# Ten gate units of a decoder layer take a fourth pair by seven products, and 15 of their weight sums are formed in the mixer

## The chip, the cores and the metric

One core of a Trainium2 chip runs one whole decoder layer. The metric is the device time of one execution in microseconds (us). TensorE (PE in the profile) multiplies, VectorE (DVE) and ScalarE (ACT) convert and combine, GpSimd (POOL) and SyncE (SP) issue most of the transfers (DMA).

## What is computed

The layer has 256 tokens of 2048 features, in float32:

```python
h = rms_norm(x, ln_mix_pre);  q, k, v (two groups of 8 heads) = split(h @ w_in)      # w_in 2048 x 6144
o = rms_norm_per_head(concat(stick_breaking(q, k, v), dilated_mixture(q, k, v, bias)))
x = x + rms_norm(o @ w_out, ln_mix_post)                                             # 2048 x 2048
g, u = split(rms_norm(x, ln_ffn_pre) @ w_gate_up)                                    # 2048 x 11264
x = x + rms_norm((silu(g) * u) @ w_down, ln_ffn_post)                                # 5632 x 2048
x = x + sigmoid(rms_norm(x, ln_pli) @ w_pli_gate) * (p @ w_pli_proj)
```

## The kernel before

**Products.** Every float32 operand of a matmul is split into a high part (`hi`, cast to fp32r by ScalarE, L107) and a low part (`lo`, what is left, subtracted by VectorE, L108). A product is then three matmuls: hi by hi, hi by lo, lo by hi. A matmul takes a stationary tile of 128 x 128 (activations) and a moving one of 128 x 512 (weights) and adds into one of eight PSUM banks.

**Weights** come by SyncE's queue into `wraw`, are cast into `whi` and subtracted into `wlo`. Each of the three names is a ring of three buffers (`wp`, L80), so a tile is written when the users of the third one before it on its ring are done.

**Stages.** The mixer projects q, k and v chunk by chunk (`Chunk`, L131; `gemm`, L177; a group of four 128-row chunks of 512 columns is 24 matmuls, L157), with the work of the heads put between by a queue of small steps: `tick` (L117), called after each two chunks, runs the next step of `pending`. Then come w_out, the FFN in three parts (units 0 to 3, 4 to 7 and 8 to 10 of the gate, each part followed by two units of w_down), and the gate of the layer embedding.

**Pairs.** From w_out on, a unit computes two halves of 512 columns for both token tiles, and goes through the rows in pairs of chunks (`Pair`, L272). A plain pair is a 2 x 2 by 2 x 2 block product in eight products, 24 matmuls. A *seven* does it in seven products of sums and differences (after Strassen and Winograd), 21 matmuls. For that the activations' differences are made once (`sT`, by `differences`, L828), and for each pair four sums of its four weight blocks (`wsum`, one buffer, L288): one add of 1024 columns (L289) and two of 512 (L291, L292) on VectorE. Three products use the weights themselves, so three of the four blocks of `wraw` are split as they are (1536 columns, a `whi` and a `wlo`); four products use the sums, which are cast in two halves (L295, L296) and subtracted (L297) into another `whi` and another `wlo`. A seven so takes two buffers of each ring. Of a unit's eight pairs, 1, 3 and 5 are sevens (`SEVENS`, L30). Pairs 6 and 7 are always plain: after pair 5 the unit's product banks are combined (a copy by ScalarE, L409, and four adds by VectorE, L410 to L413) while the last two pairs go bank by bank, each bank ending with an add (L428), then silu (L360) or the product with it (L363).

**The order of the work** on each engine is fixed when the kernel is built: a list scheduler puts the emitted instructions in order, by priorities (weights stand 200 ahead, the chain that closes a unit 1000 ahead) and its own estimate of when operands are there. The same list decides on TensorE whether, for a tile that it expects late, all hi by hi products stand ahead of the first product that needs `wlo`. On the chip each engine keeps this order and waits for semaphores.

**p**, the layer embedding, is loaded once (L721) in the mixer by SyncE, split, and kept to the end of the kernel.

Of the kernel before, what the change touches and what calls it, by code (L numbers as in the profile page):

```python
# [34 lines left out]
def kernel(
# [234 lines left out]
    sums_pool = []  # L270

    class Pair:  # L272


        def __init__(self, src, na, nb, i, seven=False, row0=0, pieces=1):
            self.i, self.seven = i, seven
            with tc.high_priority(offset=WEIGHT_AHEAD):
# [11 lines left out]
                nc.vector.tensor_tensor(  # L289
                    s[:, 0:2], raw[:, 0:1].to_broadcast([P, 2, NB]), raw[:, 1:4:2], ALU.add)  # L290
                nc.vector.tensor_tensor(s[:, 2], s[:, 0], raw[:, 3], ALU.add)  # L291
                nc.vector.tensor_tensor(s[:, 3], s[:, 2], raw[:, 2], ALU.add)  # L292
# [716 lines left out]
```

## Time and profile before

| | |
|---|---|
| median of 3 runs | 1239.58 us (1239.23 to 1240.94) |
| profiled execution: time, span | 1239.78 us, 1238.1 us |
| granted TensorE clock | 0.999 |
| DMA, mean over the span | 198 GB/s |

The profile's page comes from one execution. The busy time of an engine is given with its share of the span; a group of instructions has its line, engine, operation and tiles (out<-in), count, busy time, mean ns of one, and what ended the idle time before it; a row of the timeline has the start in us from the span's start, the duration, and in brackets the idle time before and who ended it. Rows of windows have, after start:end and the length, the busy time and count of PE, PEld (weight loads), DVE, ACT, POOL, then the granted clock, the DMA share and GB/s. Rows of waits have the total, the count and the longest. Rows of DMA issues have count, size of one and the median time from issue to landing.

### The profile page before, as it was taken

The numbers are of one execution on the slowest core, as the hardware profiler recorded it, in microseconds if no ns is written. First come the engines' busy times: TensorE is split into PE (matmuls) and PEld (weight loads), VectorE is DVE, ScalarE is ACT, GpSimd is POOL, SyncE is SP. The second block draws the span as 40 slices with busy tenths as digits, with TensorE's granted clock in tenths as the row PEclk, the third lists the DMA queues.
The fourth block names the chain that finished last, engine by engine and source line by source line (L and its number), as shares of the span: only waits on it lengthen the run. The fifth ranks groups of instructions, "written<-read, shape, count | busy, mean of one in ns | idle before, by whom it ended". The sixth has DMA issues, their size and how long they took to land.

```text
span 1238.1 us, 14380 instructions
## 1 busy us (share of the span) xinstructions
PE 1227.1 (99%) x5496; PEld 990.4 (80%) x5496; DVE 965.4 (78%) x1007; ACT 659.7 (53%) x749; POOL 32.3 (3%) x57
## 2 busy tenths in 40 slices
PE   9999999999999999999999999999999999999997
PEld 6888888888888888888788788888888888887886
DVE  6575564545668968988888798899888988888886
ACT  6654554445444756555544555555464555655553
POOL 0001000000100200000000000000000000001000
PEclk9999999999999999999999999999999999999999
DMA  9845745555557845556455555655555665657661
GB/s 339 276 147 168 255 146 162 168 170 170 191 167 251 297 152 191 182 202 227 155 193 207 181 193 204 217 170 190 205 176 198 204 222 169 245 173 241 241 202 70
DMA packets 123301, 245.11 MB, mean 198 GB/s; under 512 B 7088, under 2 KB 7392, under 8 KB 122848
## 3 DMA queue, kind: packets, MB, share of 16 engines
q1 hardware_dynamic: 120448, 232.84, 55.6%
q0 software_dynamic: 2528, 11.02, 2.4%
q8 instruction: 43, 0.70, 0.2%
q10 hardware_dynamic: 256, 0.32, 0.1%
q14 instruction: 26, 0.21, 0.0%
HBM read 238.91 MB, written 6.83 MB: 198 GB/s over the span
## 4 chain that ended last, share of the span: by engine, by line
PE 93%; DVE 3%; DMA 1%; issue 1%; ACT 1%; POOL 0%; DVEq 0%; SPq 0%; ACTq 0%; POOLq 0%
PE bank L323 65%; PE bank L157 23%; DVE wlo L108 1%; PE bank L334 1%; PE bank L575 1%; DMA wraw<-in_w_down_dram 1%; PE bank L235 1%; PE bank L545 1%; DMA wraw<-in_w_in_dram 1%; ACT whi L107 1%; DMA y_sb<-in_xT_dram 0%; PE bank L588 0%; PE bank L587 0%; PE bank L586 0%; DVE temp L428 0%
## 5 line engine op out<-in xcount | busy, mean ns | idle before, releaser
L108 DVE TENSOR_TENSOR wlo<-wraw,whi 128x2048 fp32r<-128x2048 f32 (+3 forms) x229 | 463.6, 2033 | 162.5 <-ACT whi L107 161.6
L107 ACT CAST whi<-wraw 128x2048 fp32r<-128x2048 f32 (+3 forms) x229 | 389.7, 1704 | 330.9 <-PE bank L323 213.5
L323 PE MATMUL bank<-whi,hT_hi 128*128 128x512 f32 x667 | 262.5, 397 | 0.0
L323 PE MATMUL bank<-wlo,hT_hi 128*128 128x512 f32 x667 | 261.9, 395 | 0.0
L323 PE MATMUL bank<-whi,hT_lo 128*128 128x512 f32 x667 | 261.7, 395 | 0.0
L157 PE MATMUL bank<-whi,hT_hi 128*128 128x512 f32 x384 | 156.6, 409 | 1.2 <-ACT whi L107 1.2
L157 PE MATMUL bank<-wlo,hT_hi 128*128 128x512 f32 x384 | 152.0, 396 | 0.3 <-DVE wlo L108 0.3
L157 PE MATMUL bank<-whi,hT_lo 128*128 128x512 f32 x384 | 152.0, 396 | 0.0
L323 PEld LDWEIGHTS bank<-wlo,hT_hi 128*128 128x128 f32 x667 | 125.2, 188 | 30.8 <-DVE wlo L108 0.4
L323 PEld LDWEIGHTS bank<-whi,hT_lo 128*128 128x128 f32 x667 | 125.2, 188 | 29.9
L323 PEld LDWEIGHTS bank<-whi,hT_hi 128*128 128x128 f32 x667 | 125.2, 188 | 29.8
L297 DVE TENSOR_TENSOR wlo<-wsum,whi 128x2048 fp32r<-128x2048 f32 x50 | 114.5, 2290 | 23.8 <-ACT whi L296 23.8
L323 PE MATMUL bank<-wlo,fT_hi 128*128 128x512 f32 x282 | 111.0, 396 | 1.0 <-DVE wlo L108 1.0
L323 PE MATMUL bank<-whi,fT_hi 128*128 128x512 f32 x282 | 111.0, 396 | 0.0
L323 PE MATMUL bank<-whi,fT_lo 128*128 128x512 f32 x282 | 110.8, 396 | 0.0
L157 PEld LDWEIGHTS bank<-whi,hT_lo 128*128 128x128 f32 x384 | 72.3, 188 | 17.7 <-DVE hT_lo L493 0.2
L157 PEld LDWEIGHTS bank<-whi,hT_hi 128*128 128x128 f32 x384 | 72.3, 188 | 16.8 <-ACT whi L107 1.7
L157 PEld LDWEIGHTS bank<-wlo,hT_hi 128*128 128x128 f32 x384 | 72.4, 189 | 15.1 <-DVE wlo L108 1.1
L295 ACT CAST whi<-wsum 128x1024 fp32r<-128x1024 f32 x50 | 52.6, 1052 | 41.6 <-PE bank L323 28.4
L289 DVE TENSOR_TENSOR wsum<-wraw 128x1024 f32<-128x1024 f32 x50 | 61.0, 1221 | 6.7 <-DMA wraw<-in_w_down_dram 3.1
L323 PEld LDWEIGHTS bank<-wlo,fT_hi 128*128 128x128 f32 x282 | 53.0, 188 | 14.1 <-DVE wlo L108 1.5
L323 PEld LDWEIGHTS bank<-whi,fT_hi 128*128 128x128 f32 x282 | 53.0, 188 | 12.7
(193 smaller groups left out, 1437.4 us busy)
## 6 DMA issues: line engine op xcount, KB each, us to landing
wraw<-in_w_gate_up_dram SPq DMA_DIRECT2D x176, 512.0 KB, 4.8
wraw<-in_w_down_dram SPq DMA_DIRECT2D x88, 512.0 KB, 5.2
wraw<-in_w_in_dram SPq DMA_DIRECT2D x40, 1024.0 KB, 5.2
wraw<-in_w_pli_gate_dram SPq DMA_DIRECT2D x32, 512.0 KB, 5.1
wraw<-in_w_out_dram SPq DMA_DIRECT2D x8, 1024.0 KB, 5.0
wraw<-in_w_out_dram SPq DMA_DIRECT2D x16, 512.0 KB, 4.9
wraw<-in_w_in_dram SPq DMA_DIRECT2D x14, 512.0 KB, 8.5
y_sb<-in_x_dram SPq DMA_DIRECT2D x4, 512.0 KB, 10.2
```

Of the source, the lines that this page charges most:

```text
L107: nc.scalar.copy(hi, raw)
L108: nc.vector.tensor_tensor(lo, raw, hi.bitcast(F32), ALU.subtract)
L157: nc.tensor.matmul(self.pm[t], lhsT=a[:, c, t, :], rhs=b[:, c % KG, :], start=c == 0 and a is a_hi and b is hi, stop=c == self.nk - 1 and ...
L235: nc.tensor.transpose(out=pt[:, k * P:(k + 1) * P], in_=x_sb[c][:, t, k * P:(k + 1) * P], identity=ident)
L289: nc.vector.tensor_tensor(s[:, 0:2], raw[:, 0:1].to_broadcast([P, 2, NB]), raw[:, 1:4:2], ALU.add)
L295: nc.scalar.copy(shi[:, 0:2], s[:, 0:2])
L297: nc.vector.tensor_tensor(slo, s, shi.bitcast(F32), ALU.subtract)
L323: nc.tensor.matmul(pm, lhsT=a[u], rhs=w[v], start=first and x == 0 and y == 0, stop=last and x == len(terms) - 1 and y == 2)
L334: nc.tensor.transpose(out=pt[:, c * P:(c + 1) * P], in_=f[:, c * P:(c + 1) * P], identity=ident)
L545: nc.tensor.transpose(out=pt[:, h * P:(h + 1) * P], in_=nat[:, h * P:(h + 1) * P], identity=ident)
L575: nc.tensor.matmul(out, lhsT=a[u], rhs=b[w], start=i == 0, stop=i == 2)
```

## The change

1. **A fourth seven.** The gate units 1 to 10 take pairs 1, 2, 4 and 5 as sevens, not 1, 3 and 5. `sT` has room for four. Unit 0, w_out, w_down and the last gate stay as they are.
2. **Sums formed early.** For pair 1 of units 1 to 10 and pair 4 of the even ones, 15 sets in all, the sums are formed in the mixer. `first_sums` puts six steps for each set on a second queue (`aside`), of which `tick` runs one a call: load the four blocks by two transfers on POOL's queue into half of `y_sb`; nothing; four adds of 128x512 on VectorE; a store of 1 MB on POOL's queue into memory; nothing, twice. All sets use the one buffer. In the gate units such a pair loads its sums (1 MB, SyncE) and only three blocks of its weights (0.75 MB), and has no adds; its sums lie in another order (`swap`).
3. **p is loaded twice,** by POOL's queue: in w_out for its first use and in the third part of the FFN for its second; it isn't kept between.

The diff's core (line numbers shift: L295, L296, L297 become L337, L338, L339; L289 is L331 for the units' own sums; L409 is L452; L323 is L366; L107 and L108 stay; the early adds are L289, their loads L284, their stores L303):

```diff
+GATE_SEVENS = (1, 2, 4, 5)
+FIRST_SUMS = [(j, 1) for j in range(1, DFF // NB)] + [(j, 4) for j in range(2, DFF // NB, 2)]
...
-    pT_hi = const.tile([P, 2, T, P], F32R, name="pT_hi")
-    pT_lo = const.tile([P, 2, T, P], F32R, name="pT_lo")
...
+    def load_p(pool, raw):
+
+        nc.gpsimd.dma_start(out=raw.rearrange("q (k m) -> q k m", k=2), in_=pT)
+        p_split[:] = [pool.tile([P, 2, T, P], F32R, name=f"pT_{n}") for n in ("hi", "lo")]
+        split(*(a.rearrange("q k t m -> q (k t m)") for a in p_split), raw)
...
-    pending = deque()
+    pending, aside = deque(), deque()
...
             clock[0] += 1
+            if aside:
+                aside.popleft()()
...
+    def load_pair(queue, raw, src, rows, na, nb):
+        for n0, sl in ((nb, slice(0, 4, 3)), (na, slice(1, 3))):
+            queue.dma_start(out=raw[:, sl], in_=src[rows, n0:n0 + NB].rearrange("(c q) n -> q c n", q=P))
+
+    def first_sums(buf):
+
+        def add(o, u, v):
+            nc.vector.tensor_tensor(buf[:, o], buf[:, u], buf[:, v], ALU.add)
+
+        for j, i in FIRST_SUMS:
+            def load(j=j, i=i):
+                load_pair(nc.gpsimd, buf, w_gate_up, slice(i * 2 * P, (i + 1) * 2 * P), j * NB, DFF + j * NB)
+
+            def form():
+                add(1, 0, 1)
+                add(0, 0, 3)
+                add(3, 1, 3)
+                add(2, 3, 2)
+
+            def store(j=j, i=i):
+                sums_d[j, i] = dram.tile([P, 4, NB], F32, name=f"sums{j}_{i}")
+                nc.gpsimd.dma_start(out=sums_d[j, i], in_=buf)
+
+            idle = lambda: None
+            aside.extend((load, idle, form, store, idle, idle))
...
-            self.i, self.seven = i, seven
+            self.i, self.seven, self.swap = i, seven, 1 if sums is not None else 0
...
+                if sums is not None:
+                    nc.sync.dma_start(out=raw[:, 1:3], in_=src[rows, na:na + NB].rearrange("(c q) n -> q c n", q=P))
+                    nc.sync.dma_start(out=raw[:, 3], in_=src[rows.start + P:rows.stop, nb:nb + NB])
+                else:
+                    load_pair(nc.sync, raw, src, rows, na, nb)
...
+                if sums is not None:
+                    nc.sync.dma_start(out=s, in_=sums)
+                else:
+                    nc.vector.tensor_tensor(
+                        s[:, 0:2], raw[:, 0:1].to_broadcast([P, 2, NB]), raw[:, 1:4:2], ALU.add)
+                    nc.vector.tensor_tensor(s[:, 2], s[:, 0], raw[:, 3], ALU.add)
+                    nc.vector.tensor_tensor(s[:, 3], s[:, 2], raw[:, 2], ALU.add)
...
+            wi = wi if m < 4 else wi ^ self.swap
...
-        sevens = SEVENS[np]
+        sevens = sevens or SEVENS[np]
...
-            w = Pair(src, na, nb, i, seven, row0)
+            w = Pair(src, na, nb, i, seven, row0, sums=sums.get(i))
...
-            differences(sT)
+            differences(sT, GATE_SEVENS)
...
-        def load_late():
-
-            pT_sb = y_sb[:, 0, 0:NB]
-            with tc.high_priority(offset=WEIGHT_AHEAD):
-                nc.sync.dma_start(out=pT_sb.rearrange("q (k m) -> q k m", k=2), in_=pT)
-
-            later(lambda: split(*(a.rearrange("q k t m -> q (k t m)") for a in (pT_hi, pT_lo)), pT_sb))
...
-                if grp and base:
-                    load_late()
                 q = project_T(n0, rsq, "qT", before=load_norm if first else None)
+                if first:
+                    first_sums(y_sb[:, 0].rearrange("q (s n) -> q s n", n=NB))
...
-        sT = tuple(hxp.tile([P, 4, NS, P], F32R, name=f"sT_{n}") for n in ("hi", "lo"))
+        sT = tuple(hxp.tile([P, 4, len(GATE_SEVENS), P], F32R, name=f"sT_{n}") for n in ("hi", "lo"))
...
         load_x1(xsp, 0)
+        load_p(xsp, xsp.tile([P, NB], F32, name="p_raw"))
...
-                unit_seven(hT, sT, w_gate_up, j * NB, DFF + j * NB, KC // 2, out)
+                unit_seven(hT, sT, w_gate_up, j * NB, DFF + j * NB, KC // 2, out, sevens=GATE_SEVENS,
+                           sums={i: d for (jj, i), d in sums_d.items() if jj == j})
...
             load_x2(xs2, 0)
+            load_p(xs2, temp())
```

Three places show what moves. On ScalarE, the casts at the end of gate unit 2, before (whi_3961 and whi_3992 are pairs 4 and 5, whi_4002 the sums of pair 5, whi_4038 and whi_4045 pairs 6 and 7):

```order
L107 CAST whi_3961<-wraw_3960 128x2048
L107 CAST whi_3992<-wraw_3991 128x1536
L295 CAST whi_4002<-wsum_3996 128x1024
L296 CAST whi_4002<-wsum_3996 128x1024
L107 CAST fS_hi_3314<-temp_3848 128x4x128
L107 CAST whi_4038<-wraw_4037 128x2048
L409 COPY temp_4028<-bank4_73 128x512
L107 CAST whi_4045<-wraw_4044 128x2048
```

and after (whi_4092 are the sums of pair 4, whi_4119 pair 5, whi_4129 its sums, whi_4165 and whi_4172 pairs 6 and 7):

```order
L337 CAST whi_4092<-wsum_4088 128x1024
L338 CAST whi_4092<-wsum_4088 128x1024
L107 CAST whi_4119<-wraw_4118 128x1536
L337 CAST whi_4129<-wsum_4123 128x1024
L107 CAST whi_4165<-wraw_4164 128x2048
L452 COPY temp_4155<-bank4_73 128x512
L338 CAST whi_4129<-wsum_4123 128x1024
L107 CAST whi_4172<-wraw_4171 128x2048
L107 CAST whi_4237<-wraw_4236 128x2048
```

The cast of pair 6 and the copy now stand between the two halves of pair 5's sums. In the odd units from 3 on the copy stands ahead of the cast of pair 6, and in unit 1 that cast comes behind both halves.

On TensorE, the products of pair 5 in the same unit, before (hi by hi, lo, hi by lo in turn):

```order
L323 MATMUL bank3_72<-whi_3992,sT_hi_2731 128x512
L323 MATMUL bank3_72<-wlo_3993,sT_hi_2731 128x512
L323 MATMUL bank3_72<-whi_3992,sT_lo_2732 128x512
L323 MATMUL bank2_71<-whi_4002,sT_hi_2731 128x512
L323 MATMUL bank2_71<-wlo_4003,sT_hi_2731 128x512
L323 MATMUL bank2_71<-whi_4002,sT_lo_2732 128x512
L323 MATMUL bank1_70<-whi_4002,hT_hi_2726 128x512
L323 MATMUL bank1_70<-wlo_4003,hT_hi_2726 128x512
L323 MATMUL bank1_70<-whi_4002,hT_lo_2727 128x512
L323 MATMUL bank6_75<-whi_4002,sT_hi_2731 128x512
L323 MATMUL bank6_75<-wlo_4003,sT_hi_2731 128x512
L323 MATMUL bank6_75<-whi_4002,sT_lo_2732 128x512
```

and after:

```order
L366 MATMUL bank3_72<-whi_4119,sT_hi_2846 128x512
L366 MATMUL bank3_72<-wlo_4120,sT_hi_2846 128x512
L366 MATMUL bank3_72<-whi_4119,sT_lo_2847 128x512
L366 MATMUL bank2_71<-whi_4129,sT_hi_2846 128x512
L366 MATMUL bank6_75<-whi_4129,sT_hi_2846 128x512
L366 MATMUL bank0_69<-whi_4165,hT_hi_2841 128x512
L366 MATMUL bank7_76<-whi_4165,hT_hi_2841 128x512
L366 MATMUL bank3_72<-whi_4165,hT_hi_2841 128x512
L366 MATMUL bank1_70<-whi_4129,hT_hi_2841 128x512
L366 MATMUL bank5_74<-whi_4129,sT_hi_2846 128x512
L366 MATMUL bank2_71<-wlo_4130,sT_hi_2846 128x512
L366 MATMUL bank2_71<-whi_4129,sT_lo_2847 128x512
```

Seven hi by hi products, four with pair 5's sums and three with pair 6, stand ahead of the first one that needs wlo_4130, the low half of pair 5's sums; it is so in all ten units.

On VectorE, weight splits of the mixer between the heads' normalizations and the k projection of the next group, before:

```order
L108 TENSOR_TENSOR wlo<-wraw,whi 128x2048
L600 TENSOR_SCALAR d_1471<-ssh 128x2
L608 TENSOR_SCALAR tmp<-bank_75,rs_1473 128x128 x2
L108 TENSOR_TENSOR wlo<-wraw,whi 128x2048
L552 TENSOR_TENSOR kT<-bank_73,kT 128x4x128
L552 TENSOR_TENSOR kT<-bank_74,kT 128x4x128
L108 TENSOR_TENSOR wlo<-wraw,whi 128x2048
```

and after (the adds L289 are those of the sets 10 and 11):

```order
L289 TENSOR_TENSOR y_sb<-y_sb 128x512 x4
L108 TENSOR_TENSOR wlo<-wraw,whi 128x2048
L643 TENSOR_SCALAR d_1525<-ssh 128x2
L651 TENSOR_SCALAR tmp<-bank_75,rs_1527 128x128 x2
L108 TENSOR_TENSOR wlo<-wraw,whi 128x2048
L595 TENSOR_TENSOR kT<-bank_73,kT 128x4x128
L595 TENSOR_TENSOR kT<-bank_74,kT 128x4x128
L289 TENSOR_TENSOR y_sb<-y_sb 128x512 x4
L108 TENSOR_TENSOR wlo<-wraw,whi 128x2048
```

Each set's four adds stand between splits of weights, and VectorE reaches the splits behind them only when they are done.

More of the change, by code (lines that the diff above doesn't have):

```diff
@@ L268, with __init__ @@
     pp_d = dram.tile([P, T * D // 2], F32, name="pp_d")
-    sums_pool = []
+    sums_pool, sums_d = [], {}
+    def load_pair(queue, raw, src, rows, na, nb):
[17 more added lines that the diff above has]
+            aside.extend((load, idle, form, store, idle, idle))
     class Pair:
-        def __init__(self, src, na, nb, i, seven=False, row0=0, pieces=1):
-            self.i, self.seven = i, seven
+        def __init__(self, src, na, nb, i, seven=False, row0=0, pieces=1, sums=None):
+            self.i, self.seven, self.swap = i, seven, 1 if sums is not None else 0
             with tc.high_priority(offset=WEIGHT_AHEAD):
@@ L279, in __init__ @@
                 rows = slice(row0 + i * 2 * P, row0 + (i + 1) * 2 * P)
-                for n0, sl in ((nb, slice(0, 4, 3)), (na, slice(1, 3))):
-                    nc.sync.dma_start(
-                        out=raw[:, sl], in_=src[rows, n0:n0 + NB].rearrange("(c q) n -> q c n", q=P))
+                if sums is not None:
[3 more added lines that the diff above has]
+                    load_pair(nc.sync, raw, src, rows, na, nb)
                 self.w = (hi, lo)
@@ L288, in __init__ @@
                 s = sums_pool[-1].tile([P, 4, NB], F32, name="wsum")
[L289 to L292, printed above, removed]
+                if sums is not None:
[5 more added lines that the diff above has]
+                    nc.vector.tensor_tensor(s[:, 3], s[:, 2], raw[:, 2], ALU.add)
                 split(hi[:, 1:4], lo[:, 1:4], raw[:, 1:4])
@@ L392, in unit_seven @@
     def unit_seven(aT, sT, src, na, nb, np, out, row0=0, order=(2, 4, 8, 3), base=None, dest=None, ahead=None,
-                   M=BANKS, hold=None, between=None):
-        sevens = SEVENS[np]
+                   M=BANKS, hold=None, between=None, sevens=None, sums={}):
+        sevens = sevens or SEVENS[np]
         for i in range(np - 2):
             seven = i in sevens
-            w = Pair(src, na, nb, i, seven, row0)
+            w = Pair(src, na, nb, i, seven, row0, sums=sums.get(i))
             for m in (1, 2, 3, 5, 4, 7, 6) if seven else order:
@@ L803 @@
             nc.vector.tensor_tensor(o, u, v, op)
-            split(sT[0][:, i], sT[1][:, i], o)
+            split(sT[0][:, i, 0:NS], sT[1][:, i, 0:NS], o)
         for n in range(2):
@@ L826, in temp, with differences, laid @@
         return ffn2.tile([P, NB], F32, name="temp")
-    def differences(sT):
-        yv = y_sb.rearrange("q t (i f) -> q t i f", f=NB)
-        a1, a2, a3, a4 = (yv[:, t, 0:NS, (2 + c) * P:(3 + c) * P] for t in range(T) for c in range(2))
+    def differences(sT, sevens):
+        n = len(sevens)
+        if n == 4:
+            step = sevens[2] - sevens[0]
+            yv = y_sb[:, :, sevens[0] * 2 * P:(sevens[0] + 2 * step) * 2 * P].rearrange(
+                "q t (a b c m) -> q t a b c m", a=2, b=step, m=P)[:, :, :, 0:2]
+            a1, a2, a3, a4 = (yv[:, t, :, :, c] for t in range(T) for c in range(2))
+        else:
+            yv = y_sb.rearrange("q t (i f) -> q t i f", f=NB)
+            a1, a2, a3, a4 = (yv[:, t, 0:n, (2 + c) * P:(3 + c) * P] for t in range(T) for c in range(2))
+        def laid(x):
+            return x.rearrange("q (a b) m -> q a b m", a=2) if n == 4 else x
         box = {}
@@ L836, in run @@
                 u1, v1 = box.get(u, None) if isinstance(u, int) else u, v
-                box[i] = temp()[:, 0:NS * P].rearrange("q (i m) -> q i m", m=P)
+                box[i] = laid(temp()[:, 0:n * P].rearrange("q (i m) -> q i m", m=P))
                 nc.vector.tensor_tensor(box[i], u1, v1, op)
-                split(sT[0][:, i], sT[1][:, i], box[i])
+                split(laid(sT[0][:, i]), laid(sT[1][:, i]), box[i])
             return run
@@ L847, in embed @@
     def embed(na, banks, out, loaded=None):
-        unit_plain((pT_hi, pT_lo), w_pli_proj, na, na + NB, 1, banks, out, loaded=loaded)
+        unit_plain(p_split, w_pli_proj, na, na + NB, 1, banks, out, loaded=loaded)
     proj = []
@@ L942, in normed @@
         rs.extend(token_rs(lambda t, c: x_sb[c][:, t], t) for t in range(T))
-        differences(sP)
+        differences(sP, SEVENS[8])
     unit_plain(hT, w_pli_gate, 0, NB, KC // 2, {(0, 0): 1, (0, 1): 7, (1, 0): 2, (1, 1): 6}, evac_gate(0), front=2,
```

1 line of the change is left out of this document (added).

## Prediction

> **What bounds the kernel now.** I read the busy table of the page first, then what TensorE waited for, then one stage in a window.
>
> ```profile
> span 1238.1 us, 14380 instructions
> PE 1227.1 (99%) x5496; PEld 990.4 (80%) x5496; DVE 965.4 (78%) x1007; ACT 659.7 (53%) x749; POOL 32.3 (3%) x57
> ...
> PE bank L204 <- DVE junk L201: 1.3, 1, 1.3
> PE bank L157 <- ACT whi L107: 1.2, 1, 1.2
> PE bank L323 <- DVE wlo L108: 1.0, 1, 1.0
> ...
> 200.00:300.00 100.00, 100.00 (x484) 82.02 (x483) 52.84 (x72) 47.59 (x71) 2.76 (x4) 1.00 0.51 165
> 700.00:800.00 100.00, 100.00 (x439) 80.78 (x438) 87.10 (x80) 55.90 (x50) 0.00 (x0) 1.00 0.58 196
> ```
>
> TensorE is busy all the time, at granted clock 1.00 (the column after POOL's), and its longest wait is 1.3 us. So a matmul less is time less, and a wait that is new is time more: nothing else has to give way. VectorE (DVE) is 52.84% busy in a mixer window and 87.10% in a gate window; ScalarE (ACT) about half. The profiled execution took 1239.8 us, 0.2 above the median of the runs; I sum against 1239.8. About 0.2% (2.5 us) is what a measurement can tell from no change.
>
> **Fewer matmuls.** The pitch of matmuls is read from two rows of TensorE's timeline, 48 matmuls with nothing between:
>
> ```profile
> 614.29 0.39 PE L323 MATMUL bank<-whi,fT_hi 128*128 128x512 f32 x1
> ...
> 625.25 0.40 PE L323 MATMUL bank<-whi,fT_lo 128*128 128x512 f32 x1
> ```
>
> They start 47 pitches and 10.96 us apart: 0.2333 us each. Ten pairs go from 24 matmuls to 21, 30 x 0.2333 = **-7.0 us**, all on the path. A plain pair is 5.6 us of TensorE; a seven's own weights (h) are 9 matmuls, 2.1 us, and its sums (s) 12 matmuls, 2.8 us.
>
> **The end of a gate unit.** A whi tile has three buffers, and a seven takes two of them (h and s). In a gate unit after the change the tiles follow each other as p0, h1, s1, h2, s2, p3, h4, s4, h5, s5, p6, p7, and a tile can be written when TensorE is done with the third before it. p6 so waits for s4. Before, the last seven was followed by two plain pairs as well, but what stood ahead of its h was a plain pair of 5.6 us; now it is another seven. What each step takes:
>
> ```profile
> L108 DVE TENSOR_TENSOR wlo<-wraw,whi 128x2048 fp32r<-128x2048 f32 x151 | 345.8, 2290 | 150.3 <-ACT whi L107 149.7
> L107 ACT CAST whi<-wraw 128x2048 fp32r<-128x2048 f32 x151 | 288.4, 1910 | 280.9 <-PE bank L323 168.5 <-PE bank L157 67.5 <-issue 42.4
> L297 DVE TENSOR_TENSOR wlo<-wsum,whi 128x2048 fp32r<-128x2048 f32 x50 | 114.5, 2290 | 23.8 <-ACT whi L296 23.8
> L289 DVE TENSOR_TENSOR wsum<-wraw 128x1024 f32<-128x1024 f32 x50 | 61.0, 1221 | 6.7 <-DMA wraw<-in_w_down_dram 3.1 <-DMA wraw<-in_w_gate_up_dram 1.4 <-DMA wraw<-in_w_pli_gate_dram 0.9
> L108 DVE TENSOR_TENSOR wlo<-wraw,whi 128x1536 fp32r<-128x1536 f32 x50 | 87.6, 1752 | 2.2 <-ACT whi L107 2.2
> L296 ACT CAST whi<-wsum 128x1024 fp32r<-128x1024 f32 x50 | 52.4, 1047 | 13.4 <-DVE wsum L292 13.4
> L291 DVE TENSOR_TENSOR wsum<-wsum,wraw 128x512 f32<-128x512 f32 x50 | 34.4, 688 | 0.9
> ...
> 748.66 1.91 ACT L107 CAST whi<-wraw 128x2048 fp32r<-128x2048 f32 x1 [3.08 <-issue]
> 750.48 0.57 ACT L409 COPY temp<-bank 128x512 f32<-128x512 f32 x1
> 750.95 1.91 ACT L107 CAST whi<-wraw 128x2048 fp32r<-128x2048 f32 x1
> 753.52 1.91 ACT L107 CAST whi<-wraw 128x2048 fp32r<-128x2048 f32 x1 [0.65 <-PE bank L323]
> ...
> 753.32 0.40 PE L323 MATMUL bank<-whi,hT_hi 128*128 128x512 f32 x1
> ```
>
> Of instructions back to back the next starts a little before the end: 1.82 us after a cast of 2048, 0.47 after the copy. The last rows give a release: TensorE left the seven's sums at 753.32 (the row of its next product), and the cast into that buffer starts at 753.52, 0.20 later. The other handover, from a late low half to TensorE, is seen where before's own order puts high products ahead of a low half that comes late:
>
> ```profile
> 942.98 1.05 ACT L296 CAST whi<-wsum 128x1024 fp32r<-128x1024 f32 x1 [1.87 <-DVE wsum L292]
> 944.06 2.29 DVE L297 TENSOR_TENSOR wlo<-wsum,whi 128x2048 fp32r<-128x2048 f32 x1 [1.12 <-ACT whi L296]
> ...
> 945.63 0.39 PE L323 MATMUL bank<-whi,sT_hi 128*128 128x512 f32 x1
> 945.86 0.40 PE L323 MATMUL bank<-whi,hT_hi 128*128 128x512 f32 x1
> 946.09 0.63 PE L323 MATMUL bank<-whi,sT_hi 128*128 128x512 f32 x2
> 946.56 0.40 PE L323 MATMUL bank<-wlo,sT_hi 128*128 128x512 f32 x1
> ```
>
> ACT to DVE 0.03 us, DVE to TensorE 0.21. There four high products covered the low half exactly.
>
> Now even units (2, 4, 6, 8, 10), counted from TensorE's end of s4. ACT's order, fixed when the kernel is built, is p6's cast, the copy of product 1, the second half of s5. So: release 0.20 + p6 1.82 + copy 0.47 + half of s5 1.05 + 0.03 + low half of s5 2.29 + 0.21 = 6.07 us until TensorE has s5's low half. Until then it has h5 (2.10) and the seven high products that the order puts ahead (7 x 0.2333 = 1.63): 3.73. It waits **2.3 us**, in five units 11.7. In odd units from 3 the copy stands ahead of p6's cast, and it needs the third product of h5: 0.70 + 0.20 + 0.47 + 1.82 + 1.05 + 0.03 + 2.29 + 0.21 = 6.77, less 3.73: 3.0, in four units 12.2. In unit 1 p6's cast comes after s5's, so 6.77 - 1.82 = 4.95, less 3.73: 1.2. Sum **+25 us**. Behind the waiting half of s5 stand, on DVE, p6's low half and the corner sums of the unit; TensorE's eight products after the wait (1.9 us) nearly cover p6's low half (2.29), and I put that at nothing. The lower bound is nothing, if the low halves come in time as they do in before; the upper one has the 0.4 us of p6's low half in all ten units, +29.
>
> **DVE in a gate unit.** Three adds and a third low half are added (1.22 + 0.69 + 0.69, 2.29), a loaded set takes its three adds away and a plain 2048 becomes 1536. In a unit with one loaded set that is about +1.7 us, with two about -0.8, on 87% of some 43 us. DVE isn't the bound by its rate. SP's loads of sums (1 MB) replace 0.25 MB of weights; the DMA share of 0.58 leaves room. Nothing for both.
>
> **The sums beside the mixer.** Each of 15 sets is two loads of 512 KB on POOL's queue, four adds on DVE, and a store of 1 MB, in one buffer: load, adds, store, load form one closed chain, and the adds stand at fixed places among DVE's weight splits. If the chain is slower than TensorE, DVE waits in an add, and behind it wait the splits that TensorE needs. TensorE's pace, by the splits of before ahead of which the adds of sets 2, 10, 11 and 15 stand in the new order (the two rows ahead of them are for set 1):
>
> ```profile
> 34.80 0.16 DVE L228 TENSOR_REDUCE s<-ss 128x1 f32<-128x5 f32 x1 [1.18 <-ACT junk L224]
> ...
> 38.91 1.23 DVE L108 TENSOR_TENSOR wlo<-wraw,whi 128x1024 fp32r<-128x1024 f32 x1 [0.33 <-ACT whi L107]
> ...
> 61.25 2.29 DVE L108 TENSOR_TENSOR wlo<-wraw,whi 128x2048 fp32r<-128x2048 f32 x1 [3.31 <-ACT whi L107]
> ...
> 187.71 2.29 DVE L108 TENSOR_TENSOR wlo<-wraw,whi 128x2048 fp32r<-128x2048 f32 x1 [1.54 <-ACT whi L107]
> ...
> 200.47 2.29 DVE L108 TENSOR_TENSOR wlo<-wraw,whi 128x2048 fp32r<-128x2048 f32 x1 [2.99 <-ACT whi L107]
> ...
> 258.11 2.29 DVE L108 TENSOR_TENSOR wlo<-wraw,whi 128x2048 fp32r<-128x2048 f32 x1 [1.52 <-ACT whi L107]
> ...
> x_d<-x POOLq DMA_DIRECT2D x4, 512.0 KB, 6.6
> x<-x_d POOLq DMA_DIRECT2D x4, 512.0 KB, 4.8
> ...
> y_sb<-scratch POOLq DMA_DIRECT2D x1, 1024.0 KB, 8.3
> gpost<-in_ln_mix_post_dram POOLq DMA_DIRECT2D x1, 1024.0 KB, 6.8
> ...
> 411.87 0.54 POOL L450 DMA_DIRECT2D x_d<-x  x1
> ```
>
> From set 2 to set 15 are 196.9 us for 13 steps, 15.1 each; the shortest (10 to 11) 12.8. The chain: a store of 1 MB wasn't seen; the nearest, x_d<-x, takes 6.6 at half the size in a burst of four, and I take it. A load is an issue (0.54) and 4.8. Four adds at most 0.69 each, 2.8, and 0.5 for handovers: 15.2 in all, just the mean step. TensorE has slack: a split is needed two chunks (11.2 us) after its buffer is free, and casting and splitting take 4.2, so 7.0 us can be lost before it waits. Short steps in a row use that up; I take **+4 us**. If both transfers are as the slowest rows (8.3 and 0.54 + 6.8), the chain is 18.9: 13 x 3.8 - 7.0 = +42. If both go as x<-x_d, nothing. Set 1 is separate: its load can start when the squares of t = 0 have freed the buffer (their sum is the row at 34.80), and by the slowest row for 1 MB it lands at 34.8 + 0.54 + 8.3 = 43.6. The split behind its first add, in before at 38.91, then comes 4.7 us later. TensorE's slack may cover all or none of that; I take half, as buffers of halves are nearer to their use than whole ones: **+2.5** (0 to 4.7).
>
> By the Trainium skill, "DMA: Bandwidth & Descriptors", section "Anatomy of one DMA — SWDGE (gpsimd) path", a DMA of this queue costs about 2.0 us and its bytes at 436 GB/s, which would be an estimate of 4.4 us for 1 MB; the chain would fit into the mixer and the sum be 4 us less. The rows of this trace don't agree, with 6.8 and 8.3 for 1 MB beside the weights' traffic; I go by the rows.
>
> **p loaded twice.** Two loads of 256 KB on POOL's queue and a split of 512 more; both stand where TensorE has a chunk in hand, and POOL has nothing else queued but normalizations that are later. Nothing, at worst 1 us.
>
> **Sum.** 1239.8 - 7.0 + 25.0 + 2.5 + 4 = **1264.3 us**.
>
> **The rivals.** *The low halves are in time* (0.14): ACT runs ahead of what I laid out, or a buffer is free earlier, and the seven high products cover s5's low half as four did in before. Then 1239.8 - 7.0 + 0 to 3 of the mixer: 1234, faster. For it speaks that before's waits for weights are 1.2 and 1.0 us in the whole kernel; against it, that the sum above has no free term: 6.07 of work in a row against 3.73 of products. It decides when the wait is below 0.7 us a unit. *A smaller wait* (0.13): ACT gets a lead of one cast, as it would if s4's last product came earlier in TensorE's queue than I count: 1.8 us less in each of ten units, 1264.3 - 18 = 1246. *The chain of sums bounds the mixer* (0.20): +42 in place of +4, 1302, decided when a set's transfers take over 14 us together. POOL's normalizations of the heads then queue behind loads that wait for a store, which would add to it. The forecast has 0.53.
>
> The first lies faster, its upper part and the lower part of the second within 0.2%: faster 0.13, same 0.04, slower 0.83. The range leaves out the first rival and the tail of the third: 1243 to 1302.
>
> **What would show it.** The waits of TensorE: about ten waits of 1.2 to 3 us for a low half formed from wsum (DVE wlo L339), one at the end of each of units 1 to 10, 25 us together; each of these units with 42.0 us of products (180 x 0.2333) and 2 to 3 us of waiting; 5466 matmuls in place of 5496. In the mixer: DVE's adds (L289) waiting for DMA y_sb, and TensorE's waits for wlo L108 behind them, some 6 us in all. I am wrong if those ten waits aren't there (first rival), or if the mixer ends more than 15 us later (third).

## The result and the profile after

The changed kernel takes 1297.59 us (median of 4 runs, 1294.79 to 1300.08) where the kernel before takes 1239.40 (4 runs): a ratio of 1.0468, 95% interval 1.0444 to 1.0493, 58 us slower. The forecast was 1264.3 and slower; the way was right, the size was not. The profiled execution took 1297.77 us.

The busy tables of the page, and of its slices the granted clock (a digit for 32 us; 9 is 90% or more), then what TensorE waited for:

```profile
span 1296.0 us, 14547 instructions
PE 1244.7 (96%) x5466; PEld 993.8 (77%) x5466; DVE 1010.9 (78%) x1063; ACT 674.7 (52%) x770; POOL 64.6 (5%) x104
...
PEclk9989989999999999999999999999999999999999
...
PE bank L366 <- DVE wlo L339: 14.3, 9, 1.6
PE bank L656 <- DVE qT L595: 7.9, 1, 7.9
PE bank L618 <- DVE qT L595: 6.9, 2, 5.2
PE bank L366 <- ACT whi L107: 3.5, 5, 1.1
PE bank L656 <- DVE kT L595: 2.8, 1, 2.8
PE bank L629 <- DVE tmp L651: 2.0, 1, 2.0
PE bank L656 <- DVE oT_lo L660: 1.4, 1, 1.4
...
PE bank L366 <- ACT whi L338: 1.0, 5, 0.2
```

The 30 matmuls are gone (5466 for 5496). Two kinds of wait have come. Those of L366 are in the gate units. The others are in the mixer, and they are not for weights (`wlo`, L108) but for operands of the heads: the low parts of q and k (`qT`, `kT`) and heads' normalized outputs.

Where the time went, by TensorE's first product of w_out and its first with p, the same instructions of the kernel before and of the changed one:

```profile
313.40 0.48 PE L157 MATMUL bank<-whi,oT_hi 128*128 128x512 f32 x1
...
405.88 0.48 PE L323 MATMUL bank<-whi,pT_hi 128*128 128x512 f32 x1
```

```profile
346.42 0.48 PE L167 MATMUL bank<-whi,oT_hi 128*128 128x512 f32 x1
...
438.92 0.48 PE L366 MATMUL bank<-whi,pT_hi 128*128 128x512 f32 x1
```

The mixer ends 33.0 us later, w_out adds nothing, and the rest of the kernel, 1238.1 - 405.9 = 832.2 us before, takes 1296.0 - 438.9 = 857.1: **33.0 in the mixer and 24.9 from the FFN on.** Of the 24.9, the products give -7.0.

**One wait of the mixer.** VectorE's queue at the q projection of the second group, then TensorE:

```profile
149.76 0.48 DVE L660 SCALAR_TENSOR_TENSOR oT_lo<-bank,gT,oT_hi 128x256 fp32r<-128x256 f32 x1
162.15 0.69 DVE L289 TENSOR_TENSOR y_sb<-y_sb 128x512 f32<-128x512 f32 x1 [11.92 <-DMA y_sb<-in_w_gate_up_dram]
162.76 2.28 DVE L108 TENSOR_TENSOR wlo<-wraw,whi 128x2048 fp32r<-128x2048 f32 x1
164.97 1.28 DVE L595 TENSOR_TENSOR qT<-bank,qT 128x512 fp32r<-128x512 f32 x2
...
165.70 0.69 PE L656 MATMUL bank<-ident,tmp 128*128 128x128 f32 x2 [7.89 <-DVE qT L595]
```

VectorE stands 11.9 us in a set's first add until the load lands. Behind the add are a split of weights and the low parts of q; TensorE can do without the split, but not without q's low part, and waits 7.9 us.

**The pace of the sets,** POOL's queue at set 2, a later load and the store of the last set, VectorE at set 2, the group of the early adds, and the DMA issues (size of one, median us to landing):

```profile
56.04 1.44 POOL L284 DMA_DIRECT2D y_sb<-in_w_gate_up_dram  x2 [6.42 <-DMA sums<-y_sb]
68.39 0.56 POOL L303 DMA_DIRECT2D sums<-y_sb  x1 [10.92 <-DVE y_sb L289]
73.14 1.42 POOL L284 DMA_DIRECT2D y_sb<-in_w_gate_up_dram  x2 [4.19 <-DMA sums<-y_sb]
...
151.97 1.43 POOL L284 DMA_DIRECT2D y_sb<-in_w_gate_up_dram  x2 [3.24 <-DMA sums<-y_sb]
...
296.74 0.59 POOL L303 DMA_DIRECT2D sums<-y_sb  x1 [8.52 <-DVE y_sb L289]
...
L289 DVE TENSOR_TENSOR y_sb<-y_sb 128x512 f32<-128x512 f32 x60 | 41.3, 689 | 65.8 <-DMA y_sb<-in_w_gate_up_dram 64.9
...
65.22 2.87 DVE L289 TENSOR_TENSOR y_sb<-y_sb 128x512 f32<-128x512 f32 x4 [6.83 <-DMA y_sb<-in_w_gate_up_dram]
...
y_sb<-in_w_gate_up_dram POOLq DMA_DIRECT2D x30, 512.0 KB, 5.4
sums<-y_sb POOLq DMA_DIRECT2D x15, 1024.0 KB, 4.6
```

From the store of set 2 to that of set 15 are 228.4 us, 17.6 for a set; VectorE waited 64.9 us for the loads. The chain has no slack: each load after the first starts 0.28 or 0.29 us after the store ahead of it has landed, each store 0.3 us after the last add, and in 13 of the 15 sets the first add starts within 0.12 us of the load's landing. In the mean of these 13 steps a load takes 7.5 us from its issue to the first add, from there to the store it is 4.4 us, as other work of VectorE stands between the adds of some sets, and from the store to the next load 5.7. At set 2 the parts show: from the load's issue to the first add 9.2 us (56.04 to 65.22), the adds and the handover 3.2 (to 68.39), the store until the next load 4.8 (to 73.14). At the wait above it is 10.2 us from the load's issue (151.97) to the add, and the store ahead of that load took 10.1 to land.

**The end of a gate unit,** in unit 2, where the order was shown; ScalarE, VectorE and TensorE:

```profile
564.17 1.91 ACT L107 CAST whi<-wraw 128x2048 fp32r<-128x2048 f32 x1 [1.72 <-PE bank L366]
565.98 0.57 ACT L452 COPY temp<-bank 128x512 f32<-128x512 f32 x1
566.46 1.05 ACT L338 CAST whi<-wsum 128x1024 fp32r<-128x1024 f32 x1
...
563.60 0.69 DVE L334 TENSOR_TENSOR wsum<-wsum,wraw 128x512 f32<-128x512 f32 x1
567.54 2.29 DVE L339 TENSOR_TENSOR wlo<-wsum,whi 128x2048 fp32r<-128x2048 f32 x1 [3.25 <-ACT whi L338]
...
567.56 0.50 PE L366 MATMUL bank<-whi,hT_hi 128*128 128x512 f32 x1 [0.20 <-ACT whi L338]
567.90 0.40 PE L366 MATMUL bank<-whi,sT_hi 128*128 128x512 f32 x1
569.89 0.50 PE L366 MATMUL bank<-wlo,sT_hi 128*128 128x512 f32 x1 [1.59 <-DVE wlo L339]
```

Pair 6's cast, the copy, the second half of pair 5's sums, the low half, the product: the order of the prediction. VectorE had the sums at 564.3 and stands still for 3.25 us until ScalarE has cast them.

**The clock.** Windows inside the mixer and at the end of unit 3 (the third number from the end is the granted clock), and the products there:

```profile
70.00:76.00 6.00, 4.45 (x13) 3.78 (x14) 4.54 (x6) 1.05 (x2) 1.42 (x2) 0.50 0.97 352
162.00:168.00 6.00, 2.30 (x7) 1.91 (x8) 5.78 (x7) 2.04 (x2) 0.00 (x0) 0.50 0.34 98
616.00:619.00 3.00, 3.00 (x8) 2.32 (x9) 1.99 (x1) 0.00 (x0) 0.00 (x0) 0.50 0.00 0
...
615.84 0.78 PE L366 MATMUL bank<-wlo,sT_hi 128*128 128x512 f32 x1 [1.59 <-DVE wlo L339]
616.42 0.63 PE L366 MATMUL bank<-whi,sT_lo 128*128 128x512 f32 x1
616.85 0.63 PE L366 MATMUL bank<-wlo,hT_hi 128*128 128x512 f32 x1
```

After the wait the pitch is 0.43 us, not 0.23. So a wait that such a drop follows costs more than its length.

### The profile page after: what moved, and what is told of

It is laid out like the page before. It is cut to its first block, busy times and chain, and to the rows that moved or that the text cites. A ratio compares the mean times of both kernels' runs of the same rounds, so it can differ in the third digit from the quotient of the medians.

```text
span 1296.0 us, 14547 instructions
## 1 busy us (share of the span) xinstructions
PE 1244.7 (96%) x5466; PEld 993.8 (77%) x5466; DVE 1010.9 (78%) x1063; ACT 674.7 (52%) x770; POOL 64.6 (5%) x104
## 5 line engine op out<-in xcount | busy, mean ns | idle before, releaser
L107 ACT CAST whi<-wraw 128x2048 fp32r<-128x2048 f32 (+3 forms) x229 | 385.0, 1684 | 308.8 <-PE bank L366 161.0
L108 DVE TENSOR_TENSOR wlo<-wraw,whi 128x2048 fp32r<-128x2048 f32 (+3 forms) x229 | 458.5, 2008 | 69.5 <-ACT whi L107 68.9
L366 PE MATMUL bank<-whi,hT_hi 128*128 128x512 f32 x617 | 243.7, 401 | 4.5 <-ACT whi L107 3.5
L366 PE MATMUL bank<-wlo,hT_hi 128*128 128x512 f32 x617 | 243.8, 398 | 0.0
L366 PE MATMUL bank<-whi,hT_lo 128*128 128x512 f32 x617 | 243.3, 397 | 0.0
L339 DVE TENSOR_TENSOR wlo<-wsum,whi 128x2048 fp32r<-128x2048 f32 x60 | 137.4, 2290 | 57.3 <-ACT whi L338 57.2
L167 PE MATMUL bank<-whi,hT_hi 128*128 128x512 f32 x384 | 159.5, 416 | 1.3 <-ACT whi L107 0.7
L167 PE MATMUL bank<-wlo,hT_hi 128*128 128x512 f32 x384 | 155.0, 404 | 0.3 <-DVE wlo L108 0.3
L167 PE MATMUL bank<-whi,hT_lo 128*128 128x512 f32 x384 | 154.8, 403 | 0.0
L366 PEld LDWEIGHTS bank<-whi,hT_hi 128*128 128x128 f32 x617 | 116.5, 189 | 37.7 <-ACT whi L107 5.7
L366 PEld LDWEIGHTS bank<-wlo,hT_hi 128*128 128x128 f32 x617 | 116.9, 189 | 29.6 <-DVE wlo L108 1.8
L366 PEld LDWEIGHTS bank<-whi,hT_lo 128*128 128x128 f32 x617 | 116.7, 189 | 28.0
L366 PE MATMUL bank<-whi,fT_hi 128*128 128x512 f32 x282 | 111.0, 396 | 0.0
L366 PE MATMUL bank<-wlo,fT_hi 128*128 128x512 f32 x282 | 110.9, 395 | 0.0
L366 PE MATMUL bank<-whi,fT_lo 128*128 128x512 f32 x282 | 110.8, 396 | 0.0
L337 ACT CAST whi<-wsum 128x1024 fp32r<-128x1024 f32 x60 | 63.2, 1053 | 57.6 <-DVE wsum L331 29.0
L289 DVE TENSOR_TENSOR y_sb<-y_sb 128x512 f32<-128x512 f32 x60 | 41.3, 689 | 65.8 <-DMA y_sb<-in_w_gate_up_dram 64.9
L167 PEld LDWEIGHTS bank<-whi,hT_lo 128*128 128x128 f32 x384 | 74.0, 193 | 18.3 <-DVE hT_lo L536 0.2
L167 PEld LDWEIGHTS bank<-whi,hT_hi 128*128 128x128 f32 x384 | 74.3, 194 | 17.6 <-ACT whi L107 1.2
L167 PEld LDWEIGHTS bank<-wlo,hT_hi 128*128 128x128 f32 x384 | 74.2, 193 | 15.8 <-DVE wlo L108 1.1
L366 PE MATMUL bank<-wlo,sT_hi 128*128 128x512 f32 x172 | 71.8, 417 | 14.3 <-DVE wlo L339 14.3
L338 ACT CAST whi<-wsum 128x1024 fp32r<-128x1024 f32 x60 | 63.0, 1049 | 20.5 <-DVE wsum L334 20.5
```

The costliest lines, as they stand in the source:

```text
L107: nc.scalar.copy(hi, raw)
L108: nc.vector.tensor_tensor(lo, raw, hi.bitcast(F32), ALU.subtract)
L167: nc.tensor.matmul(self.pm[t], lhsT=a[:, c, t, :], rhs=b[:, c % KG, :], start=c == 0 and a is a_hi and b is hi, stop=c == self.nk - 1 and ...
L289: nc.vector.tensor_tensor(buf[:, o], buf[:, u], buf[:, v], ALU.add)
L337: nc.scalar.copy(shi[:, 0:2], s[:, 0:2])
L338: nc.scalar.copy(shi[:, 2:4], s[:, 2:4])
```

## The experiments

Theory: two causes that have nothing to do with each other. In the mixer, VectorE held in an early add; in the gate, the order on ScalarE at pair 5 with a ring of three; and behind each wait the clock. Rivals: the traffic of the early sums, POOL's queue, loaded sums that are late, VectorE's load.

**e1_no_early: no early sums.**

```diff
-FIRST_SUMS = [(j, 1) for j in range(1, DFF // NB)] + [(j, 4) for j in range(2, DFF // NB, 2)]
+FIRST_SUMS = []
```

> The changed kernel with no sums formed in the mixer: every seven of a gate unit forms its own sums on VectorE. My theory (the mixer's 33 us are VectorE waiting in the early adds for their chain of transfers, the gate's 25 us are the ring and ScalarE's order at pair 5 with the clock drops that follow): the mixer ends where it ended before, w_out's first product at 313 us and not at 346; the gate units lose at least the 32 us that they lose in the changed kernel, and more since VectorE has up to 2.6 us of adds more in each of 15 pairs on an engine that is nearly full: 1264 + 5 to 25, so 1269 to 1290 us. Rival (the gate's waits come from loaded sums that are late): with no loaded sums they go, 1240 - 7 = 1233 us.

1297.91 us (ratio 1.0477, 1.0459 to 1.0494), as slow as the changed kernel, with w_out's first product at 313.3 us. The mixer's loss is the early sums, all of it. The rival on late loads falls: without loaded sums the rest of the kernel is not 25 us slower but 58. The amount was above my 1269 to 1290. TensorE waits at pair 2 now too, for its low half and for pair 3's cast, which I had not counted, and longer at pair 5. The 15 sets save 34 us in the gate and cost 33 in the mixer.

**e2_mixer_only: early sums formed and stored, not loaded; gate units as before.**

```diff
-GATE_SEVENS = (1, 2, 4, 5)
+GATE_SEVENS = (1, 3, 5)
...
-                unit_seven(hT, sT, w_gate_up, j * NB, DFF + j * NB, KC // 2, out, sevens=GATE_SEVENS,
-                           sums={i: d for (jj, i), d in sums_d.items() if jj == j})
+                unit_seven(hT, sT, w_gate_up, j * NB, DFF + j * NB, KC // 2, out, sevens=GATE_SEVENS)
```

> The early sums are formed and stored in the mixer as in the changed kernel, but nobody loads them: the gate units take pairs 1, 3 and 5 as before. My theory: the whole mixer loss and nothing of the gate's, 1239 + 33 = 1272 us, w_out's first product at 346 us, no wait of TensorE over 1.2 us after it. Rival (part of the mixer's loss is given back later, or p's two loads cost): away from 1272 by more than 4 us.

1269.38 us (1.0256, 1.0241 to 1.0272): 31 us slower than before, and w_out's first product at 344.4. The mixer's loss stands alone, and p's two loads cost nothing that shows.

**e3_no_adds: e2 without the adds.** It leaves out the four adds of each set.

```diff
-            aside.extend((load, idle, form, store, idle, idle))
+            aside.extend((load, idle, idle, store, idle, idle))
```

> As e2_mixer_only, with the loads and the stores but without the four adds of a set; the stored sums are then the weights themselves, and nobody uses them. My theory (VectorE stands in an add until the load lands, and the heads' work queued behind the add is what TensorE waits for): with no add in VectorE's queue nearly all of the 33 us go, 1239 to 1244 us. Rival (the 3 MB more of traffic for each set slow the weights' loads): the loss stays, over 1260 us. Second rival (POOL's queue: the heads' normalizations stand behind loads that wait for a store): a loss of 5 to 15 us stays, as waits for POOL's rs.

1282.52 us (1.0346, 1.0323 to 1.0369), slower than with the adds: my theory's number is off by 40 us. What TensorE waited for, and POOL's queue at the first of the two waits:

```profile
PE bank L629 <- DVE tmp L651: 21.4, 1, 21.4
PE bank L629 <- DVE d L643: 17.9, 1, 17.9
...
111.76 0.57 POOL L303 DMA_DIRECT2D sums<-y_sb  x1 [4.19 <-DMA y_sb<-in_w_gate_up_dram]
116.25 0.70 POOL L284 DMA_DIRECT2D y_sb<-in_w_gate_up_dram  x1 [3.91 <-DMA sums<-y_sb]
116.97 0.72 POOL L228 TENSOR_TENSOR rs<-d,mhalf 128x2 f32<-128x2 f32 x1
```

A head's normalization (`rs`) comes on POOL behind loads and stores that wait for each other, and two such waits are 39 of the 44 us. The second rival was right in kind, and far too small in size. The run cannot tell the adds from the traffic, since taking the adds away moved the loss to another queue. So both were taken apart:

**e7_no_adds_act: e3 with the heads' normalization on ScalarE.**

```diff
-            r = rsqrt(d2, T)
+            r = small.tile([P, T], F32, name="rs2")
+            nc.scalar.activation(out=r, in_=d2, func=AF.Ln)
+            nc.scalar.activation(out=r, in_=r, func=AF.Exp, scale=-0.5)
```

> As e3_no_adds (loads and stores of the early sums, no adds, gate units with pairs 1, 3 and 5), with the heads' reciprocal square roots taken from GpSimd to ScalarE (exp of -0.5 ln), so that in the mixer nobody waits for anything behind POOL's queue of transfers except the bias. My theory (order, not traffic: in e3 two heads' normalizations stood 18 and 21 us behind loads on POOL's queue): the loss of e3 goes, 1238 to 1244 us. Rival (45 MB of traffic beside the weights slow the mixer): 1255 us or more, with waits of ScalarE's casts for the weights' transfers.

1238.70 us, no different from before (0.9999, 0.9990 to 1.0008). A window of its mixer:

```profile
100.00:200.00 100.00, 99.45 (x478) 80.59 (x477) 56.06 (x68) 52.04 (x86) 16.59 (x25) 1.00 0.94 335
```

The transfers move 335 GB/s with the DMA 94% busy, and TensorE is busy all the same. The traffic by itself costs TensorE nothing, and the rival on traffic falls; what the traffic does to the length of a load or a store counts only where something waits for it.

**e10_adds_act: e2 with the same three lines,** the adds back on VectorE.

> The control to e7: e2_mixer_only (sums formed by VectorE and stored, nobody loads them) with the heads' reciprocal square roots on ScalarE, as in e7. So e2, e3, e7 and e10 are the four cases of adds or none, POOL or ScalarE. My theory (VectorE held by an add is what costs): the loss of e2 stays, 1258 to 1270 us. Rival (it was POOL's queue of normalizations all along, in e2 too): 1245 us or less.

1266.83 us (1.0218, 1.0201 to 1.0235). With the normalization off POOL the adds still cost 27 us: it is VectorE's queue. So the loss is 31 us with the adds and the normalization on POOL (e2), 44 without the adds (e3), 27 with the adds and the normalization on ScalarE (e10), and nothing with neither (e7). The waits are in part for other things than in e2 (q's and k's low parts 10 us, ScalarE's `sps` and `nat` 8), because the order of ScalarE changed with the edit.

**e4_later_adds: other spacing of the six steps.**

```diff
-            aside.extend((load, idle, form, store, idle, idle))
+            def form_store(form=form, store=store):
+                form()
+                store()
+
+            aside.extend((load, idle, idle, idle, form_store, idle))
```

> The changed kernel with another spacing of the same six steps of a set: load, nothing three times, adds and store in one step, nothing. The load has four steps (about 11 us of products) in place of two, the store two in place of three. My theory: a load takes 8 to 9.5 us from its issue to the last landing, so the adds then hardly wait; the mixer's loss falls from 33 to under 10 us: 1265 to 1275 us, w_out's first product before 323 us. Rival (the closed chain is too long for the mixer whatever the spacing): still over 340 us at w_out, 1290 us or more.

1297.47 us (1.0475, 1.0459 to 1.0490), as the changed kernel, with the same waits at the same products (8.3 and 7.1 us for q's low parts). VectorE does its work of the mixer in the same sequence, instruction by instruction. It seems that the list scheduler takes an add as soon as it expects the load to have landed, wherever the program emits it. The theory isn't tested by this; the edit didn't move what it was meant to move.

**e8_pool_adds: e7 with the four adds, on GpSimd.**

```diff
-            nc.vector.tensor_tensor(buf[:, o], buf[:, u], buf[:, v], ALU.add)
+            nc.gpsimd.tensor_tensor(buf[:, o], buf[:, u], buf[:, v], ALU.add)
```

> As e2_mixer_only (sums formed and stored in the mixer, nobody loads them), with the four adds on GpSimd, behind its own loads, and the heads' reciprocal square roots on ScalarE as in e7. My theory (the loss is VectorE's queue held by an add that waits): no add in VectorE's queue, 1238 to 1246 us where e2 had 1269. Rival (GpSimd's adds slow VectorE's work, or are too slow for 15 sets): VectorE's means grow by over 10%, or the store of set 15 comes after the mixer's end; over 1250 us.

1277.43 us (1.0312, 1.0296 to 1.0327), slower than with VectorE's adds; my theory's number fails, and the rival is right in its second part. The adds, and VectorE when the mixer ends:

```profile
L289 POOL TENSOR_TENSOR y_sb<-y_sb 128x512 f32<-128x512 f32 x60 | 97.2, 1620 | 79.1 <-DMA y_sb<-in_w_gate_up_dram 75.6
...
327.91 0.56 DVE L838 TENSOR_TENSOR y_sb<-oT_hi,oT_lo 128x384 f32<-128x384 f32 x1 [31.41 <-DMA sums<-y_sb]
```

An add takes 1.62 us in the mean on GpSimd (1.28 where VectorE does nothing beside it) and 0.69 on VectorE. The last store comes so late that VectorE's first work for w_out, which needs the buffer, waits 31 us for it, and 21 us of TensorE's waits are there. Another 4.9 us come from a transfer of the heads (`lines_d`) on POOL's queue. So no run here forms the sums beside the mixer without a loss.

**e5_last_on_dve: one cast moved in the changed kernel,** the second half of pair 5's sums from ScalarE to VectorE.

```diff
-                nc.scalar.copy(shi[:, 2:4], s[:, 2:4])
+                (nc.vector.tensor_copy if last else nc.scalar.copy)(shi[:, 2:4], s[:, 2:4])
...
-            w = Pair(src, na, nb, i, seven, row0, sums=sums.get(i))
+            w = Pair(src, na, nb, i, seven, row0, sums=sums.get(i), last=i == 5 and len(sevens) == 4)
```

> The changed kernel with one cast moved: the second half of pair 5's sums is cast by VectorE (1024 columns, about 1.2 us) and not by ScalarE, where pair 6's cast and the copy stand ahead of it. My theory (that order on ScalarE holds pair 5's low half, and the waits it makes drop the clock): in even units VectorE has the sums 2 us earlier than ScalarE could cast them, and the wait goes from 2.1 us to under 0.5; in odd units from 2.5 to about 1.1; most of the clock drops go too. 32 us of loss in the gate become 6 to 12: 1297 - 20 to 26 = 1271 to 1277 us, w_out's first product still at 346 us. Rival (VectorE itself is the bound at pair 5, or the loss follows from the ring wherever the cast is made): no gain, or a loss, 1295 us or more.

1271.51 us (1.0263, 1.0240 to 1.0286): 26 us less than the changed kernel, by one instruction of ten units. Of the profiled executions' difference 23.2 us are from p's first product on, where the edit is; the other 3.5 are in the mixer, which the edit leaves as it is. (With 15 early sets on VectorE w_out's first product comes anywhere from 337.8 us, in e9, to 347.0, in e4.) VectorE in unit 2:

```profile
562.88 0.69 DVE L334 TENSOR_TENSOR wsum<-wsum,wraw 128x512 f32<-128x512 f32 x1
563.68 0.69 DVE L338 CAST whi<-wsum 128x1024 fp32r<-128x1024 f32 x1
564.48 2.29 DVE L339 TENSOR_TENSOR wlo<-wsum,whi 128x2048 fp32r<-128x2048 f32 x1
...
PE bank L366 <- DVE wlo L339: 5.1, 7, 1.7
```

Sums, cast and low half follow each other on one engine; the cast takes 0.69 us, not the 1.2 that I expected. Of 18.8 us of gate waits (14.3, 3.5 and the 1.0 of L338) 5.3 are left: 2.4 in unit 2, where the load of pair 4's sums landed late, 0.6 in each of units 3, 5, 7 and 9, and 0.5 in unit 1. In the FFN the clock no longer drops. The gate's loss is 833.8 - 832.2 + 7.0 = 8.6 us, within the theory's 6 to 12; the time was in its range with the help of the mixer's 3.5. From its first product with p (435.5) to the end of the span it takes 833.8 us, against 832.2 before: the -7.0 are eaten by what is left.

**e9_1234: sevens 1, 2, 3, 4.**

```diff
-GATE_SEVENS = (1, 2, 4, 5)
-FIRST_SUMS = [(j, 1) for j in range(1, DFF // NB)] + [(j, 4) for j in range(2, DFF // NB, 2)]
+GATE_SEVENS = (1, 2, 3, 4)
+FIRST_SUMS = [(j, 1) for j in range(1, DFF // NB)] + [(j, 3) for j in range(2, DFF // NB, 2)]
```

> The changed kernel with pairs 1, 2, 3 and 4 as sevens, pair 5 plain, and the early sums for pairs 1 and 3 (even units). As many matmuls and early sums. My theory (a buffer is free when TensorE has done the third chunk before; a plain pair is 5.6 us of cover, a seven's halves 2.1 and 2.8): pair 6 now has a plain pair ahead of it, but pairs 3 and 4 have sevens ahead and one of them forms its sums late: two waits of 1 to 3 us a unit in place of one, 1300 to 1325 us. Rival (it is only the end of a unit, with its copy and pair 6's cast, that makes the wait): the waits go with the plain pair 5, 1270 us or less.

1351.45 us (1.0923, 1.0901 to 1.0946). TensorE no longer waits for pair 6, but for pairs 3 and 4, and for pair 5's cast. The rival's number falls, its idea is not settled: the copy and a plain pair's cast now stand around pair 4's sums on ScalarE as they stood around pair 5's (in unit 2 the copy at 564.94, the first half at 565.42, pair 5's cast at 566.37, the second half at 568.17), so the run moved that order and did not take it away. My theory had the way right and the size too small by 26 us: sevens in a row cost still more than I had thought.

**e11_pool_1_4 and e12_pool_1_4a: no early sums, GpSimd adds in the gate units.** Both have e5's cast and `FIRST_SUMS = []`. In e11 GpSimd makes all adds of pairs 1 and 4, in e12 those of pair 1 and the first add of pair 4.

```diff
+                    by = [nc.gpsimd if k in aux else nc.vector for k in range(3)]
-                    nc.vector.tensor_tensor(
+                    by[0].tensor_tensor(
                         s[:, 0:2], raw[:, 0:1].to_broadcast([P, 2, NB]), raw[:, 1:4:2], ALU.add)
-                    nc.vector.tensor_tensor(s[:, 2], s[:, 0], raw[:, 3], ALU.add)
-                    nc.vector.tensor_tensor(s[:, 3], s[:, 2], raw[:, 2], ALU.add)
+                    by[1].tensor_tensor(s[:, 2], s[:, 0], raw[:, 3], ALU.add)
+                    by[2].tensor_tensor(s[:, 3], s[:, 2], raw[:, 2], ALU.add)
```

> No early sums at all: in the gate units the sums of pairs 1 and 4 are formed by GpSimd, which is idle there (adds of 512 columns took it 1.62 us, so a set some 6.5 us), and the second half of pair 5's sums is cast by VectorE as in e5. Pairs 1, 2, 4 and 5 are sevens. My theory (the mixer's loss is the early adds alone, and the gate's is VectorE's and ScalarE's order around pairs 2 and 5): the mixer ends at 313 us, and the gate keeps a part of its 7 us: 1233 to 1242 us. Rival (GpSimd is too slow: between pair 2's low half and pair 4's cast are about 4 us for 6.5 us of adds): waits for pair 4's sums of 2 to 3 us a unit, 1255 us or more.

> As e11, but of pair 4's sums GpSimd makes only the first add (1024 columns, about 3.2 us) and VectorE the other two. My theory: less wait for pair 4's sums than in e11 if GpSimd is too slow there, and 1 us more of VectorE's time ahead of pair 5: 1235 to 1250 us. Rival (VectorE isn't relieved enough): waits at pair 5 as in the odd units of e5 in all ten, 1250 us or more.

1277.32 us (1.0310, 1.0294 to 1.0325) and 1253.31 us (1.0117, 1.0102 to 1.0132): both lie in their rivals' ranges, e12 3 us above my theory's. The mixer is as before. In e11 GpSimd's three adds take 3.25, 2.08 and 1.55 us, and TensorE waits 33 us, 30 of them at pairs 4 and 5. For pair 4's sums it waits 1.3 us in eight units, less than the rival had; more is lost behind them, for a reason that neither theory nor rival had. GpSimd and VectorE at pair 4 of unit 2 in e11:

```profile
520.60 4.38 POOL L332 TENSOR_TENSOR wsum<-wraw 128x1024 f32<-128x1024 f32 x1 [15.01 <-DVE wlo L340]
522.65 3.96 DVE L108 TENSOR_TENSOR wlo<-wraw,whi 128x1536 fp32r<-128x1536 f32 x1
```

The split of 1536 columns takes 1.75 us in the fifty cases without an add of GpSimd beside it, and 3.95 in the median of the ten with one: 20 us more of VectorE's time. VectorE's sums that read a PSUM bank (L473, 0.69 us) take no longer beside GpSimd's adds. No version of the fourth seven that was run beats the kernel before.

## Why the prediction was right in its direction and wrong in its size

**Fewer matmuls, -7.0:** right; 5466 are left.

**The end of a gate unit, +25.0:** right in mechanism and nearly in size. Beyond the pitch TensorE lost 2.13 us in unit 2 (1.76 at the low half's product and 0.37 ahead of it), 2.5 in unit 3 and 1.2 in unit 1, where the prediction had 2.3, 3.0 and 1.2; over the ten units 22 us. e5 shows that it is the order on ScalarE. Not in the sum was the clock: 24.9 + 7.0 - 22 leaves about 10 us, some 7 of it in the five drops that the waits set off in the gate units: in the 5 us behind the low half's product TensorE falls 1.65 us behind the pitch in the units with a drop, and 0.1 to 0.2 in the others. That these windows' low clock follows the waits is seen in the trace, and their going with the waits in e5.

**DVE in a gate unit, nothing:** right as long as the sets are loaded; e1 shows what it is without them.

**The sums beside the mixer, +4 and +2.5:** this is the step that failed: 33.0 us. Two of its parts were wrong. The pace: I had 15.2 us for a set, with 5.3 for the load (0.54 + 4.8), 3.3 for the adds and handovers and 6.6 for the store; the sets came every 17.6, with 7.5, 4.4 and 5.7. I had priced the load as one transfer of 512 KB; it is two, with an issue of 0.7 us each and the weights' transfers beside them. VectorE's other work between the adds was not counted. The store took less than I took, 4.6 in the median, but up to 10.1. And the slack: 7.0 us was that of a weight split, but behind the adds stand also q's and k's low parts, for which TensorE has no chunk in hand. The sign that I named, waits for `wlo` (L108), did not come. From set 2 to set 15 the mixer took 228.4 - 196.9 = 31.5 us longer than before, nearly all of the 33.0. TensorE's waits are 22.7 us of it, at a few places and not spread; most of the rest is the clock, which stood at 0.50 for 23.9 us of the mixer. The third rival, the chain of sums as the bound of the mixer, is what happened, at 33 in place of 42; it had 0.20. Its condition, over 14 us for a set's transfers, was not quite met (some 13): the part of the adds made up for it. The set-1 term came to nothing: VectorE waited for that load until 42.6, and TensorE did not wait between 15 and 66 us.

**p loaded twice, nothing:** right (e2, e7).

**The Trainium skill** ("DMA: Bandwidth & Descriptors", section "Anatomy of one DMA — SWDGE (gpsimd) path") had 4.4 us for 1 MB: the stores took 4.6 in the median, close to it and nearer than my 6.6. The loads, in two pieces beside the weights, took 7.5 us in the mean to the first add; a fixed time and the bytes do not make that up, and the sum by this price was further off than mine.

**The chances:** slower by over 0.2% had 0.83 and came. The range up to 1302 held the time, because it reached to the third rival, and in part by luck: that rival had some 12 us too much for the mixer (42 + 2.5 against 33.0) and some 7 too little for the gate, where the clock was not in the sum.

## What to carry to other kernels

An add that waited for a transfer here cost what the operand behind it that was needed soonest cost, not the slack of the main stream: look for who else is queued behind an instruction that waits. A price of "hidden work" is then a price of order and not of rate, and moving one short instruction to the engine that already holds its operand can be worth more than the saved products (23 us against 7 here). Where taking one suspect away makes it slower, the queue behind it was the next in line; take both away and then put each back.
